# An encoder layer on one core: the pair-wise output projection with squares, root, gate and sums at other steps, and the second FFN product with its left operands in one line and its loads in a set order

## The chip, the cores and the metric

The kernel runs on one core of one Trainium2 chip. A core has five engines that run side by side, each through its own list of instructions in order: TensorE (PE, matmuls; its weight loads are shown apart as PEld), VectorE (DVE), ScalarE (ACT), GpSimd (POOL) and SyncE (SP), which in this kernel issues nearly all transfers between the chip's memory and the on-chip memory. They wait for one another through semaphores. The metric is the device time of one execution in microseconds (us). Before the change it is 2302.77 us, the median of three runs (2301.56 to 2306.2).

## The reference

One layer of a bidirectional encoder over 2048 rows of 1024 numbers, in float32. Cut to the two parts that matter here:

```python
    mix = jnp.concatenate([att, h_m], axis=-1) @ w_out          # output projection
    x = x + gate1 * mix

    hff = rms_norm(x, g_norm2) * (1.0 + scale2) + shift2
    gte, up = jnp.split(hff @ w_ffn_in, 2, axis=-1)             # first FFN product
    ff = (jax.nn.silu(gte) * up) @ w_ffn_out                    # second FFN product
    x = x + gate2 * ff
    return rms_norm(x, g_final)
```

`att` is the attention's output, divided by its root mean square (row by row) ahead of the product; `h_m` is the mLSTM's output times a gate. The inner width of the FFN is 2816.

## The kernel before

Every float32 product is made of three passes of the array: each operand is split into a high part (ACT copies it, rounded) and a low part (DVE subtracts the high part from the original), and `mm3` (lines 55 to 58) issues high x high, high x low and low x high. On top of it the three large products use the Strassen-Winograd scheme: the two operands are cut into 2 x 2 blocks, and seven products of sums of blocks replace eight. The sums are named A11, A12, S1 to S4, A22 on one side and B11, B21, B22, T1 to T4 on the other. Nearly all engine work below is the making of such sums and of their high and low parts, just ahead of the matmuls that use them.

**The order of the work** is written out by hand for the output projection and the first FFN product: inside `manual_schedule` the instructions of an engine stand in the order in which the Python code issues them. The context `rest` holds DVE, ACT, POOL and SP that way; it is closed in the second FFN product, behind the loop of its first product A11. From there on a planner orders these four engines: it may pull an instruction forward when its inputs are ready by its own reckoning. PE keeps its written order to the end (context `hand`).

**The output projection** (loop from line 1439) goes through the 16 row tiles of 128 rows in 8 pairs, p = 0 to 7. For a pair the seven products of 12 matmuls each make 84 matmuls, given out in 28 steps `i` of three (`pull(1)`); product u covers steps 4u to 4u + 3, and when its last matmul is issued DVE adds the result to the residual rows `xr` (line 1178). A bank of products u = 0, 2, 4 and 6 is the same one, likewise that of 3 and 5, so such an addition must be done before the product after the next one may start. Beside the matmuls of a pair (`cur`) the loop does, at set steps: for the following pair (`nxt`) the scaling of the attention rows (`scale`, i = 1), the gate (`gate`, DVE), the sums (`sums`, `s1`, `s4`, POOL), the high parts (`hi`, ACT, at the steps in `HI`) and the low parts (`lo`, DVE, at the steps in `LO`); for the pair after that (`nx2`) the squares of the attention rows (`square`: ACT, then POOL folds them into `msq`), their column sums on PE (`columns`, bank `aps`), the reciprocal root (`rsqrt`, twelve small DVE instructions) and the diagonal matrix from it; and for the finished pair before (`prev`, only for p = 1 to 4) the scaling of its rows with the same root (`prev.scale`, ACT), their transposes on PE (`trn`) at steps 16 to 23 and, for pairs 2 and 3, the sums of the first FFN product's right side (DVE and POOL at steps 20 and 25). `dl` is 1 in pairs 4 and 5, where two instructions of the pair before were put off into this one, and 0 in the others. Behind an `x1` row, `hop_d` and the attention buffer `ma` stand transfers by SP.

**The first FFN product** (`pair`, units n = 0 to 43, two halves of the rows of 22 units each) makes, per unit, seven products of 12 matmuls. Beside product u the generator `weights` makes the next unit's seven weight sums in seven parts; `STEPS[u]` says how many parts are made behind product u. ACT's queue holds, in order, the splits of these parts, the copies of the unit's own banks (`s`, `u`, `c`) and the tanh. Units 0 and 22 start a half; there the right side's last operands are also split beside the products (`finish_op`).

**The second FFN product** (from line 1645) has seven products u in the order A11, S2, S3, A22, S1, S4, A12, each with 11 steps k over the inner width. A step takes one left operand (128 x 1024, loaded from `a_d` by `raw_a`, split by `split_a`, lines 1671 and 1672) and one right operand (`op_w`, POOL sums and a split, lines 1680 and 1681), and has 8 x 3 matmuls into eight banks. The last two steps of a product (seven for A12) are done bank by bank (`tail`), so that DVE can empty one bank after another (`evac`). The left operands live in a ring of four pairs of tiles, so a load waits for the matmuls of the operand four before it. In A11 the loads are written out three ahead (`raw_`), from A11's step 1 on, behind `stores()`, which issues the last five stores to `a_d`; in the other products the code loads an operand where it uses it (`load_a`) and the planner pulls it forward. The weights' blocks come in as W11, W12, W22 and later W21 (`load_w2`, `load_w21`).

In product S1 the residual rows `x1` of one half of the row tiles are loaded (`x1_row`, two tiles) and added (`row0`, line 1811), in S4 those of the other half (`row1`, line 1797), whose rows are then finished: squares, root, two scalings (line 1803) and the store to the output (line 1804). A12's tail finishes the first half's rows (lines 1815 to 1839).

Of the kernel before, what the change touches and what calls it, by code (L numbers as in the profile page):

```python
# [21 lines left out]
P = 128  # L22
T = 2048
D = 1024
# [12 lines left out]
def hybrid_layer_kernel(  # L37
# [1398 lines left out]
    HI, LO = (5, 12, 17, 19, 21, 23, 25), (5, 13, 18, 20, 22, 24, 26)  # L1436
    FIRST = (1, 2, 5, 8, 16, 20, 24)
    rows = None
    for p in range(NPR):
# [15 lines left out]
        for i in range(28):  # L1455
# [27 lines left out]
            if nx2:  # L1483
                if i == 2:
                    sq = [(xd.tile([P, 512], F32, tag="n2", name="msq", bufs=9) if p else
                           w1.tile([P, 512], F32, tag="sq", name="msq")).rearrange("p (k t) -> p k t", k=4) for _ in range(2)]
                    for j in range(2):
                        nx2.square(j, sq[j])
                if i == 8 + dl:
                    ps = bank("a", "aps")  # L1490
                    for j in range(2):
                        columns(ps, j, sq[j])
# [10 lines left out]
            if nx2 and i == 9 + dl:  # L1503
                parts = [(ps[:, :2], 2, 512)] + ([(prev.ssq, 2, D)] if prev else [])
                r = rsqrt(mx, parts, 2 * len(parts), None, f"ar{len(parts)}")
                nx2.diagonal(r, diag())
            if nxt:
                if i == 11:
                    nxt.gate()
                if i == 12:  # L1510
                    nxt.sums(ms2())
                if i == 15:
                    nxt.s1()
                if i == 16:
                    nxt.s4()
            if prev:
                if i == 11:
                    prev.scale(r[:, 2:4])
                prev.step(i)
# [12 lines left out]
    with tc.tile_pool(name="ff", bufs=1, side="right", reuse_waits="tile") as ff:  # L1532
# [91 lines left out]
        for n, (hh, j) in enumerate(units[:-1]):  # L1624
            ws_, turn = nxt_w, n == NJ - 1
            start = lambda u: None
            if turn:
                hop1, finish_op, start = refill_ops(1)
                assert not norms
            STEPS = (0, 0, 0, 2, 2, 1, 2) if n in (0, NJ) else (0, 0, 1, 1, 2, 2, 1)  # L1630

            def beside(u):

                nonlocal nxt_w, raw, more_w
                if n == 0 and u < 3:
                    finish_op(u + 4)
                if n == NJ and u < 2:
                    finish_op(u + 5)
                if turn:
                    if u > 1:  # L1640
                        finish_op(u - 2)
                    return
                if u == 1:
                    more_w = weights(raw)
                for _ in range(STEPS[u]):
                    nxt_w = next(more_w)
                if wseq and (u == 6 and n != NJ - 2 or u == 0 and n == NJ):
                    raw = load_raw(wseq.popleft())
                if n > 1 and u in (1, 3, 5) and norms and next(norms[0], None) is None:
                    norms.popleft()  # L1650

            pair(hh, j, ws_, hop, start, beside)
            if turn:
                hop = hop1
# [29 lines left out]
        W2 = [{}, {}, {}]  # L1684
# [24 lines left out]
        def op_w(u, k):  # L1709
# [8 lines left out]
            if u == "S3":  # L1718
                r = split_w(x1_)
                load_w21(k)  # L1720
                return r
# [9 lines left out]

        def operands(u, k):
            return load_a(u, k), op_w(u, k)

        g2h = wp.tile([P, D], F32, tag="wraw", name="g2h", bufs=1)
        early, raw_, todo_ = [], [], iter(range(KH))

        def split_early():
            k = next(todo_)
            early.append((split_a(*raw_[k]), op_w("A11", k)))  # L1740

        def first_operands(u):

            if u in (1, 3, 5):
                raw_.append(raw_a("A11", len(raw_)))
# [9 lines left out]
        raw_.append(raw_a("A11", 0))  # L1755
# [3 lines left out]
        stores()  # L1759
# [9 lines left out]

        def x1_row(tt, slot):  # L1770
            t = big(slot, "x1r", (P, D), F32)
            sp.dma_start(t, x1_d[tt * P:(tt + 1) * P, :])
            return t
# [18 lines left out]
        def row1(i):  # L1792

            tt = TO[8 * (i // 4) + 4 + i % 4]
            xr = x1_row(tt, i % 2)
            z = rb[i]
            dve.tensor_tensor(z, z, xr, ADD)
# [6 lines left out]
            sp.dma_start(out[tt * P:(tt + 1) * P, :], z)  # L1804
# [3 lines left out]
        def row0(i):  # L1808

            xr = x1_row(TO[8 * (i // 4) + i % 4], i % 2)  # L1810
            dve.tensor_tensor(ra[i], ra[i], xr, ADD)  # L1811
# [32 lines left out]
        for u in ("A11", "S2", "S3", "A22", "S1", "S4", "A12"):  # L1844
# [11 lines left out]
            for k in range(KH - KL):  # L1856
                a, w = early.pop(0) if early else operands(u, k)
                if u == "A11":
                    if k and k + 3 < KH:
                        raw_.append(raw_a("A11", k + 3))  # L1860
                    if k + 2 < KH:
                        load_w2(W12, k + 2)
                    for k_ in (k,) if k < 8 else range(8, KH):
                        load_w2(W22, k_)
# [8 lines left out]
            if u == "A12":  # L1873
                aring.extendleft([("ff", "xt")] * 2 + [("big", f"big{i}") for i in (1, 0, 27, 26, 25, 24)])
            if u == "A11":
                rest.close()
            tail = [early.pop(0) if early else operands(u, k) for k in range(KH - KL, KH)]
            for i in range(8):
                for k, (a, w) in enumerate(tail):
                    mms(i, KH - KL + k, a, w)  # L1880
                evac(u, i, ps[i])
        hand.close()
# [29 lines left out]
```

## Time and profile before

| | |
|---|---|
| median of three runs | 2302.77 us |
| the profiled execution | 2303.92 us |
| its span, first to last instruction | 2302.1 us |
| PE busy | 2230.1 us, 97% of the span, 10822 matmuls |
| DVE busy | 1635.1 us, 71% |
| ACT busy | 1061.6 us, 46% |
| POOL busy | 1057.7 us, 46% |
| output projection, first to last matmul | about 843.7 to 1018.7 us |
| first FFN product | 1018.7 to 1871 us |
| second FFN product | 1871 to 2294 us |

The products of the second FFN product begin at about 1871 (A11), 1931 (S2), 1991 (S3), 2053 (A22), 2113 (S1), 2175 (S4) and 2235 us (A12).

How to read the lines: a row of the order of time has the start, the length, the engine, the line of the kernel, the operation, the tiles as output<-inputs, their shapes and, in brackets, how long the engine had been idle and what ended it. SPq is SP issuing a transfer: the row's length is the issuing, not the transfer. A row of waits has the waiting instruction, what it waited for, and the sum, the number and the longest of these waits. Matmuls overlap in the array: each one lasts about 0.39 us, and they start 0.227 us apart where nothing is missing, so a wait shows as a larger distance between two starts.

### The profile page before, as it was taken

To read this page: it belongs to the slowest core of one execution; us is meant where nothing else is said; L and a number is where in the kernel's file an instruction comes from. 1 tells how busy PE (TensorE), PEld (TensorE's weight loads), DVE (VectorE), ACT (ScalarE), POOL (GpSimd) and SP (SyncE) were. 2 spreads that over 40 slices of the span, in tenths; PEclk is the share of its full clock that TensorE was granted. 3 is DMA by queue.
4 is the path that set the end of the run, shared out by engine and by line. 5 is a ranking of instruction groups with operands and counts; after the bars stand their busy time and mean duration, and the time that the engine had idled before them with its cause. 6 is when DMAs were issued, how large, how long until landed. Compare 5 with 4: busy or idle time off the path is not lost.

```text
span 2302.1 us, 32525 instructions
## 1 busy us (share of the span) xinstructions
PE 2230.1 (97%) x10822; PEld 1859.8 (81%) x10822; DVE 1635.1 (71%) x2995; ACT 1061.6 (46%) x2206; POOL 1057.7 (46%) x876
## 2 busy tenths in 40 slices
PE   6999999999999999999999999999999999999998
PEld 4997778788788878788888888788888878888887
DVE  6787577667687887886667786766666656685694
ACT  5433555545487855444444443533333333233452
POOL 1006534334234343626656666466665654592020
PEclk9999999999999999999999999999999999999999
DMA  8476745577665666863343443533333374443462
GB/s 327 160 246 211 251 149 172 163 220 206 186 186 176 196 213 209 275 247 133 110 148 128 145 160 126 181 118 98 110 105 108 99 266 140 159 155 101 139 218 91
DMA packets 355499, 393.38 MB, mean 171 GB/s; under 512 B 21388, under 2 KB 253180, under 8 KB 355332
## 3 DMA queue, kind: packets, MB, share of 16 engines
q1 hardware_dynamic: 355108, 391.28, 52.3%
q8 instruction: 85, 1.39, 0.2%
q14 instruction: 82, 0.67, 0.1%
q10 hardware_dynamic: 224, 0.04, 0.0%
HBM read 272.05 MB, written 119.19 MB: 170 GB/s over the span
## 4 chain that ended last, share of the span: by engine, by line
PE 51%; DVE 3%; DMA 2%; issue 1%; ACT 1%; POOL 0%; SPq 0%; ACTq 0%; POOLq 0%; DVEq 0%
PE fp L56 12%; PE fp L57 12%; PE fp L58 11%; PE fo L58 5%; PE fo L57 5%; PE fo L56 5%; DMA al<-a_d 1%; PE ops L56 1%; PE ops L57 1%; PE ops L58 1%; DVE al L1672 1%; DVE ra L1811 0%; DVE w L1681 0%; PE trn L166 0%; DMA T<-hop_d 0%
## 5 line engine op out<-in xcount | busy, mean ns | idle before, releaser
L466 PE MATMUL gps<-hT,whi 128*128 128x512 f32 x1088 | 397.5, 419 | 0.3 <-DVE cacc L500 0.3
L57 PE MATMUL fo<-w,ah 128*128 128x512 f32 x616 | 239.9, 389 | 1.9 <-DVE w L1681 1.9
L58 PE MATMUL fo<-w,al 128*128 128x512 f32 x616 | 240.0, 390 | 0.8 <-DVE al L1672 0.8
L56 PE MATMUL fo<-w,ah 128*128 128x512 f32 x616 | 239.8, 389 | 0.0
L466 PE MATMUL gps<-hT,wlo 128*128 128x512 f32 x544 | 228.6, 420 | 0.0
L466 PEld LDWEIGHTS gps<-hT,whi 128*128 128x128 f32 x1088 | 202.0, 191 | 24.5 <-DVE cacc L500 0.7
L56 PE MATMUL fp<-T,S 128*128 128x512 f32 x528 | 206.9, 392 | 2.9 <-ACT s L1568 2.9
L57 PE MATMUL fp<-T,S 128*128 128x512 f32 x528 | 205.7, 390 | 0.0
L58 PE MATMUL fp<-T,S 128*128 128x512 f32 x528 | 205.4, 389 | 0.0
L1672 DVE TENSOR_TENSOR al<-al,ah 128x1024 fp32r<-128x1024 f32 x77 | 120.4, 1568 | 111.0 <-ACT ah L1671 110.9
L1671 ACT ACTIVATE ah<-al 128x1024 fp32r<-128x1024 f32 x77 | 81.7, 1062 | 189.7 <-DMA al<-a_d 185.1
L1411 DVE TENSOR_TENSOR S<-sf,S 128x512 fp32r<-128x512 f32 x86 | 129.4, 1542 | 36.8 <-ACT S L1410 36.6
L1411 DVE TENSOR_TENSOR A<-graw,A 128x512 fp32r<-128x512 f32 x86 | 130.2, 1536 | 16.1 <-ACT A L1410 16.0
L1576 DVE SCALAR_TENSOR_TENSOR g<-t,g 128x512 f32<-128x512 f32 x44 | 44.0, 1000 | 131.0 <-ACT t L1575 131.0
L58 PE MATMUL fp<-B,A 128*128 128x512 f32 x352 | 136.9, 389 | 0.0
L56 PE MATMUL fp<-B,A 128*128 128x512 f32 x352 | 136.9, 389 | 0.0
L57 PE MATMUL fp<-B,A 128*128 128x512 f32 x352 | 136.9, 389 | 0.0
L57 PEld LDWEIGHTS fo<-w,ah 128*128 128x128 f32 x616 | 115.6, 188 | 26.3 <-DVE w L1681 2.2
L58 PEld LDWEIGHTS fo<-w,al 128*128 128x128 f32 x616 | 115.6, 188 | 25.8 <-DVE al L1672 1.7
L56 PEld LDWEIGHTS fo<-w,ah 128*128 128x128 f32 x616 | 115.6, 188 | 24.2 <-ACT w L1680 0.3
L758 POOL TENSOR_SCALAR ap<-ap,adn 128x384 f32<-128x384 f32 (+1 forms) x128 | 73.4, 593 | 125.9 <-DVE adn L756 53.1
L1415 POOL TENSOR_TENSOR sf<-A,A22r 128x512 f32<-128x512 f32 x43 | 59.1, 1374 | 156.1 <-DMA A22r<-in_w_ffn_in_dram 145.7
(419 smaller groups left out, 6201.3 us busy)
## 6 DMA issues: line engine op xcount, KB each, us to landing
al<-a_d SPq DMA_DIRECT2D x77, 512.0 KB, 3.7
wmod<-in_w_mod_dram SPq DMA_DIRECT2D x48, 512.0 KB, 6.8
graw<-in_w_ffn_in_dram SPq DMA_DIRECT2D x43, 512.0 KB, 3.9
a_d<-ka SPq DMA_DIRECT2D x66, 256.0 KB, 4.7
bc<-bc_d SPq DMA_DIRECT2D x64, 256.0 KB, 4.0
hop_d<-n SPq DMA_DIRECT2D x56, 256.0 KB, 4.4
a_d<-u SPq DMA_DIRECT2D x55, 256.0 KB, 4.7
mqk<-qk_d SPq DMA_DIRECT2D x48, 256.0 KB, 4.3
```

The source lines that it names most:

```text
L56: pe.matmul(o, lh, rh, start=first, stop=False, skip_group_check=skip)
L57: pe.matmul(o, lh, rl, start=False, stop=False, skip_group_check=skip)
L58: pe.matmul(o, ll, rh, start=False, stop=last, skip_group_check=skip)
L466: pe.matmul(ps, w[i == 2][:, k, :], hT[n](i == 1, k), start=(k == 0 and i == 0), stop=(k == KT - 1 and i == 2))
L758: pool.tensor_scalar(self.p[g][:, :self.NK], self.p[g][:, :self.NK], dn[:, g:g + 1], 0.0, MUL, ADD)
L1411: dve.tensor_tensor(t[:, 1, :], f, t[:, 0, :].bitcast(F32), SUB)
L1415: pool.tensor_tensor(f1, a21, a22, ADD)
L1576: dve.scalar_tensor_tensor(g0, t0, 1.0, g0, ADD, MUL)
L1671: act.activation(ah, al.bitcast(F32), AF.Copy)
L1672: dve.tensor_tensor(al, al.bitcast(F32), ah.bitcast(F32), SUB)
```

## The change

In the output projection the steps of several helpers are moved; in the first FFN product `STEPS` of units 0 and 22; in the second FFN product the left operands come from one iterator over all products (`line`), fetched by `fetch` at written places, three steps ahead; the W22 loads and the stores of the last unit are moved within A11; SP gets a written order to the end of the kernel (`manual_schedule` on SP behind A11's loop); and for this the loads of W21, the stores of finished rows and the loads of the residual rows, which the code issued from inside their users, are collected and issued by `rows_of` ahead of a step. The number of instructions and of transfers stays as it is.

```diff
-    HI, LO = (5, 12, 17, 19, 21, 23, 25), (5, 13, 18, 20, 22, 24, 26)
+    HI, LO = (5, 14, 18, 20, 22, 24, 26), (5, 14, 19, 21, 23, 25, 27)
...
-                if i == 2:
+                if i == 2 + 4 * dl:
...
                     for j in range(2):
                         nx2.square(j, sq[j])
-                if i == 8 + dl:
+                if i == 8 + 2 * dl:
                     ps = bank("a", "aps")
-                    for j in range(2):
-                        columns(ps, j, sq[j])
+                if i in (8 + 2 * dl, 9 + 2 * dl):
+                    columns(ps, i - 8 - 2 * dl, sq[i - 8 - 2 * dl])
...
-            if nx2 and i == 9 + dl:
+            if nx2 and i == 10 + 2 * dl:
...
-                if i == 11:
+                if i == 12:
                     nxt.gate()
-                if i == 12:
+                if i == 13:
                     nxt.sums(ms2())
-                if i == 15:
+                if i == 16:
                     nxt.s1()
-                if i == 16:
+                if i == 17:
                     nxt.s4()
             if prev:
-                if i == 11:
+                if i == 12:
                     prev.scale(r[:, 2:4])
...
-            STEPS = (0, 0, 0, 2, 2, 1, 2) if n in (0, NJ) else (0, 0, 1, 1, 2, 2, 1)
+            STEPS = (0, 0, 0, 1, 1, 2, 3) if n in (0, NJ) else (0, 0, 1, 1, 2, 2, 1)
...
             if u == "S3":
-                r = split_w(x1_)
-                load_w21(k)
-                return r
+                put_back.append(k)
+                return split_w(x1_)
...
+        US = ("A11", "S2", "S3", "A22", "S1", "S4", "A12")
+        line, raw_ = iter([(u, k) for u in US for k in range(KH)]), deque()
+
+        def fetch(n=1):
+
+            for u, k in islice(line, n):
+                if (u, k) == ("A12", 4):
+                    aring.extendleft([("ff", "xt")] * 2 + [("big", f"big{i}") for i in (1, 0, 27, 26, 25, 24)])
+                raw_.append(raw_a(u, k))
+
         def operands(u, k):
-            return load_a(u, k), op_w(u, k)
+            return split_a(*raw_.popleft()), op_w(u, k)
...
         pair(1, JO[0], nxt_w, hop, then=first_operands)
-        stores()
...
+        def rows_of(u, k):
+
+            while put_back:
+                load_w21(put_back.pop(0))
+            while outs:
+                sp.dma_start(*outs.pop(0))
+            if u in ("S1", "S4"):
+                for i in (0, 1) if k == 0 else (k,) if 1 < k < 8 else ():
+                    x1_row(TO[8 * (i // 4) + 4 * (u == "S4") + i % 4], i % 2)
...
-            sp.dma_start(out[tt * P:(tt + 1) * P, :], z)
+            outs.append((out[tt * P:(tt + 1) * P, :], z))
...
             for k in range(KH - KL):
+                if u != "A11" or k:
+                    fetch(2 if u == "A12" else 1)
+                rows_of(u, k)
                 a, w = early.pop(0) if early else operands(u, k)
                 if u == "A11":
-                    if k and k + 3 < KH:
-                        raw_.append(raw_a("A11", k + 3))
                     if k + 2 < KH:
                         load_w2(W12, k + 2)
-                    for k_ in (k,) if k < 8 else range(8, KH):
+                    if k == 2:
+                        stores()
+                    for k_ in ((), (), (), (0, 1), (2, 3), (4,), (5, 6), (7, 8), (9, 10))[k]:
                         load_w2(W22, k_)
...
             if u == "A11":
                 rest.close()
+                hand.enter_context(tc.manual_schedule(engines={mybir.EngineType.SP}))
+            if u != "A12":
+                fetch()
+            rows_of(u, KH)
             tail = [early.pop(0) if early else operands(u, k) for k in range(KH - KL, KH)]
             for i in range(8):
                 for k, (a, w) in enumerate(tail):
                     mms(i, KH - KL + k, a, w)
                 evac(u, i, ps[i])
+            if u != "A12":
+                fetch()
```

## The prediction made before the run

> **What bounds the kernel now.** I read the page first (TensorE, PE, is busy 97% of the span and the chain that ended last runs through PE for most of its length), then the busy times of chosen stretches, then PE's waits from the output projection on, and last the order of time around each wait. The stretches below are the output projection; the start of the first FFN product; its turn to the second half; product S3 of the second FFN product; its product S4. Columns: stretch, length, then busy time of PE, PE's weight loads, DVE, ACT, POOL.
>
> ```profile
> 843.70:1018.70 175.00, 169.49 (x788) 137.95 (x789) 138.61 (x255) 85.42 (x140) 77.47 (x64) 1.00 0.70 235
> 1018.70:1048.00 29.30, 27.82 (x121) 22.37 (x120) 26.87 (x25) 13.63 (x21) 11.77 (x7) 1.00 0.44 150
> 1447.70:1479.00 31.30, 27.76 (x120) 21.98 (x119) 25.90 (x26) 15.79 (x23) 16.91 (x10) 1.00 0.49 168
> 1991.00:2053.00 62.00, 61.18 (x268) 49.91 (x268) 53.30 (x35) 17.53 (x22) 56.40 (x32) 1.00 0.55 188
> 2173.00:2235.00 62.00, 62.00 (x275) 51.36 (x274) 60.01 (x138) 36.68 (x60) 7.65 (x6) 1.00 0.69 239
> ```
>
> PE is idle 5.5, 1.5, 3.5 and 0.8 us in the first four, and never in S4, where 62.00 us for 275 matmuls give 0.23 us from start to start: that is the pace to beat. All that an edit here can take away are PE's waits after 843.7 us (last column but two: total, times, longest):
>
> ```profile
> PE fp L56 <- ACT s L1568: 2.9, 3, 1.2
> PE aps L1081 <- POOL msq L1033: 2.5, 3, 0.9
> PE fp L56 <- ACT c L1579: 2.1, 2, 1.3
> PE fo L57 <- DVE w L1681: 1.9, 1, 1.9
> PE ops L56 <- DVE xr L1178: 1.8, 3, 0.9
> PE ops L56 <- ACT mA L1070: 1.2, 2, 1.0
> PE fo L58 <- DVE al L1672: 0.8, 2, 0.5
> ```
>
> They sum to 13.2 us of 2302.1. So the change is worth a few us either way; what a measurement can tell from no change is about 0.2%, 4.6 us.
>
> **Second FFN product, first left operands.** The wait of 1.9 us stands here, in product A11 at step 4 (a step is 24 matmuls, 24 x 0.227 = 5.44 us):
>
> ```profile
> 1879.29 1.62 POOL L1613 TENSOR_TENSOR ka<-ka,g 128x512 f32<-128x512 f32 x1
> ...
> 1880.94 0.32 SPq L1545 DMA_DIRECT2D a_d<-ka  x1
> ...
> 1883.27 0.38 SPq L1667 DMA_DIRECT2D al<-a_d  x1
> ...
> 1891.19 1.06 ACT L1671 ACTIVATE ah<-al 128x1024 fp32r<-128x1024 f32 x1 [15.19 <-DMA al<-a_d]
> ...
> 1892.82 0.49 PE L56 MATMUL fo<-w,ah 128*128 128x512 f32 x1
> 1895.24 0.50 PE L57 MATMUL fo<-w,ah 128*128 128x512 f32 x1 [1.92 <-DVE w L1681]
> ```
>
> SP sat in the stores of the last unit until POOL had finished them (1880.9), so the load of step 4's operand went out at 1883.27, landed at 1891.2 (7.9 us) and the split came late: 1895.24 - 1892.82 - 0.23 = 2.2 us lost. The change puts this load ahead of the stores (they move to step 2) and of the W22 loads (the first two go at step 3). Its tile is free when PE ends step 0, at 1892.8 - 3 x 5.44 = 1876.5. The usual time to landing is in this row of the DMA issues (size, median us):
>
> ```profile
> al<-a_d SPq DMA_DIRECT2D x77, 512.0 KB, 3.7
> ```
>
> With 3.7 to 7.9 us the operand is there at 1880 to 1884.5, and with 1.1 us of ACT and at most 4 us of DVE split by 1889.5: **-2.2 us**, from 0 (if DVE, in order, stands behind something else) to -2.2. The W22 loads start some 5 us later than now; they feed the POOL sums of S2, a whole product away. The stores, now behind operand 5 in SP's queue, are read back only at steps 9 and 10; nothing waits.
>
> **The same, later products.** SP gets a set order to the end. Today the planner pulls the residual adds that belong to S1 into S2 and S3, as these rows in order of time show:
>
> ```profile
> 2000.27 2.32 DVE L1811 TENSOR_TENSOR ra<-ra,x1r 128x1024 f32<-128x1024 f32 x1
> 2002.51 2.32 DVE L1672 TENSOR_TENSOR al<-al,ah 128x1024 fp32r<-128x1024 f32 x1
> ```
>
> The add stands ahead of the split that PE waits for (the 0.8 us of the last row of waits). With the x1 loads issued in S1 the adds cannot run in S3: **-0.8 us**. A rule of the Trainium skill bears on this (SBUF — State Buffer, "Who interferes with whom"): a VectorE instruction with two SBUF inputs contends with a GpSimd one that reads SBUF. The 2.32 us here, with POOL busy 56.40 of 62 us, agree; by it the adds get cheaper still in a product without POOL work, which changes nothing in the sum, since DVE does not bind there.
>
> **S4 and the single queue.** This is what the set order can cost. In S4, SP's list per step is now: left operand three ahead, store of row i-2, x1 load of row i. The store waits for the whole row (add, square, root, two scalings), and everything behind it waits too. The rows of today, first the add and the store with first and last start, then the x1 loads' time to landing:
>
> ```profile
> L1797 DVE TENSOR_TENSOR rb<-rb,x1r x8: 1216/1219/1224, 2166.1 to 2202.0; 128x1024 f32<-128x1024 f32 x8
> L1804 SPq DMA_DIRECT2D out_dram<-rb x8: 337/338/338, 2179.2 to 2216.8; - x8
> DMA to landing us min/median/max: 3.8/5.6/8.0
> ```
>
> From add to store it is 13.1 us for the first row and 14.8 for the last, on a DVE that is 97% busy (60.01 of 62.00). Undisturbed it is far less; a half row in the last product's tail:
>
> ```profile
> 2284.62 0.69 DVE L1815 TENSOR_TENSOR ra<-ra,fo 128x512 f32<-128x512 f32 x1 [0.64 <-PE fo L58]
> ...
> 2288.01 0.75 DVE L1838 SCALAR_TENSOR_TENSOR ra<-ra,fry,gfb 128x512 f32<-128x512 f32 x1
> ```
>
> 4.1 us; a whole row has 0.5 more add, some 0.4 more square and a second scaling of 0.75: about 5.8, an estimate from these rows. Call the time from landing to store c. From S4's start the x1 loads of rows 0 and 1 go at 1 us; row 2's load goes behind row 0's store, row 4's behind row 2's, row 6's behind row 4's: at 1 + 3 x 5.6 + 3c = 17.8 + 3c. Behind it stands the last left operand, needed at 9 x 5.44 + 0.7 = 49.7 and landing plus split is 3.7 + 1.1 + 1.2 = 6.0: so it is late once c exceeds **8.6 us**, by 3 us for each us more. c lies between 5.8 and 14.8. I take 9.1, a little under the middle, since part of today's load on DVE are splits for the last product, whose loads now come later: **+1.5 us**, ends 0 and +18.
>
> **The steps of the weights.** In the first unit of each half the splits of the next weights move later (0,0,0,2,2,1,2 to 0,0,0,1,1,2,3), so that DVE's add and ACT's tanh of the unit come ahead of two of them. Two of the three waits of 2.9 us end on the copy s of the following unit, which stands in ACT's queue behind those splits:
>
> ```profile
> 1472.47 1.75 POOL L1422 TENSOR_TENSOR graw<-graw,sf 128x512 f32<-128x512 f32 x1
> ...
> 1475.86 0.58 ACT L1568 ACTIVATE s<-fp 128x512 f32<-128x512 f32 x1
> 1476.49 0.50 PE L56 MATMUL fp<-T,S 128*128 128x512 f32 x1 [1.09 <-ACT s L1568]
> ```
>
> At 1476 POOL ends the last sum at 1474.2; two splits that need it or come behind it, of some 0.5 us each, and then s follow in either order, so s could start at 1475.3 instead of 1475.9 at best. Of the 1.1 us I take 0.3, since a sum of the unit now goes ahead of two of these on POOL. In the first half, where POOL is ahead, I take the whole wait, 2.9 - 1.1 - 1.2 = 0.6 (the third is the turn itself, untouched, and so are the 2.1 us at c): **-0.9 us**, from +0.5 (g of the next unit later) to -1.7.
>
> **Output projection.** A step here is three matmuls, 0.68 us. The column sums are split over two steps, the root comes one step later (two in pairs 4 and 5, where the squares also move four steps), gate, sums, scale one step, and the low halves now stand behind the residual adds on DVE. Rows of pair 4, second column sum, scaling of the rows, their transposes:
>
> ```profile
> 942.07 0.27 PE L1081 MATMUL aps<-ones_r,msq 128*128 128x1 f32 x1 [0.83 <-POOL msq L1033]
> ...
> 945.29 2.19 ACT L1252 ACTIVATE xr<-xr,ar2y 128x1024 f32<-128x1024 f32 x2 [5.24 <-DVE ar2y L106]
> 947.28 0.80 PE L1269 MATMUL trn<-ident,xr 128*128 128x128 f32 x4
> ```
>
> From the column to the scaled rows it is 947.5 - 942.1 = 5.4 us, and the transposes stay at step 16. In pair 4 the second column now stands behind step 11: five steps, 3.4 us, are left, so PE waits 5.4 - 3.4 = 2.0 us there; today it arrives at 947.28, some 0.2 us early: +1.8. In pairs 1 to 3 seven steps, 4.8 us, are left: 0 to 0.6 each, taken as +0.2 in all. In pair 5 the gate comes out about 1 us later against the residual add that PE waits for: +0.8. The waits for msq (2.5) are in pairs 1, 4 and 5: in 4 and 5 the squares go up to four steps later and the columns only one and two, so they keep most of theirs; -1.0, ends 0 and -2.5. The residual adds ahead of the low halves: of the 1.8 + 1.2 us I take -0.7, because the load of a later pair's ma is released by such a low half, and pair 1's columns then wait for it. Sum **+1.1 us**, ends -5.5 (every projection wait gone) and +3.5.
>
> **Sum:** -2.2 - 0.8 + 1.5 - 0.9 + 1.1 = -1.3 us. On the profiled execution's 2303.92 us (span 2302.1, the rest before and after it) that is 2302.6; it lay 1.15 us above the median 2302.77, so of the median **2301.4 us**. Likeliest case alone: 2297.5 to 2306. Chance 0.40.
>
> **Rivals.** (1) **SP's queue in S4 decides.** From c of about 10.5 us the loss there is 5.7 us or more: at 11, 7.2 us instead of 1.5, so 2307.1; at 14.8, 18.6, so 2318.5. For it: the add-to-store times of today; against: the splits of the last product leave DVE. Chance 0.27. In a sentence apart: the Trainium skill (TensorE: Matmul & The Clock Gate, "What's actually happening") has PE fall to half its clock after an idle window of 3.4 us, which would add an estimated 1.7 us to such a stall; no wait here after 843.7 us is that long, and the clock column reads 1.00. (2) **All waits go.** The projection loses its 5.5 us, S4 none: -3.0 - 0.9 - 5.5 = -9.4, so 2293.4; with half of the projection's, 2296. Against it the 5.4 us from column to rows in pair 4. Chance 0.23. (3) **The loads gain nothing**: operand 4 lands in time, but DVE's order lets another split be late, and S3 stays: -0.9 + 1.1 + 1.5 = +1.7, 2304.5; for it, DVE works in order and is busy 53.30 of 62 us in S3. Chance 0.10.
>
> **Numbers.** Faster by over 0.2%: 0.23 of (2) and 0.04 of the likeliest, 0.27. Slower: 0.27 of (1), 0.04 of (3), 0.03 of the likeliest, 0.34. Within: 0.39. The range, 2295.5 to 2311.5, leaves out the ends of (1) and (2).
>
> **What would show it.** Right: no wait of PE at A11's step 4, the operand's load issued near 1876.5; no row add between S2 and S3; a wait of about 2 us at pair 4's first transposes; PE waiting briefly, or not, at S4's tail with the last al load behind a store. Wrong: a wait of over 6 us there (rival 1), no wait at all in the projection (rival 2), or a new wait in S2, A22 or A12, where I see none.

## The result, and the profile after

The changed kernel takes **2313.4 us** in the median of four runs (2313.04 to 2314.46), the kernel before 2302.28 us beside it: a ratio of 1.0046, interval 1.0028 to 1.0063. It is slower by 0.46%; the forecast was 2301.4 us and its range ended at 2311.5. The profiled execution took 2313.04 us (span 2311.3), 9.1 us more than that of before.

To see where, I cut both traces at the first matmul of each stretch. The windows of the changed kernel: projection, then A11, S3, S4 and A12 of the second FFN product (columns as in the prediction; the last three are the granted clock, the DMA share and GB/s).

```profile
845.17:1021.25 176.08, 169.94 (x788) 137.50 (x789) 136.62 (x255) 85.58 (x140) 73.59 (x64) 1.00 0.70 233
1873.01:1932.85 59.84, 59.84 (x266) 49.55 (x264) 39.58 (x32) 17.94 (x23) 46.99 (x27) 1.00 0.65 218
1992.69:2052.53 59.84, 59.84 (x266) 49.55 (x264) 37.01 (x30) 18.61 (x23) 49.27 (x30) 1.00 0.41 137
2172.21:2234.83 62.62, 60.41 (x266) 49.40 (x264) 53.31 (x122) 30.16 (x49) 4.18 (x4) 1.00 0.62 218
2234.83:2303.14 68.31, 63.62 (x265) 51.05 (x263) 46.56 (x108) 25.17 (x43) 7.48 (x5) 0.95 0.32 124
```

And A12 of the kernel before:

```profile
2233.94:2293.99 60.05, 60.05 (x265) 49.35 (x263) 33.50 (x90) 18.78 (x34) 5.33 (x4) 1.00 0.27 97
```

| stretch, us | before | after | difference | forecast |
|---|---|---|---|---|
| ahead of the projection (code unchanged) | 843.7 | 845.2 | +1.5 | 0 |
| output projection | 175.0 | 176.1 | +1.1 | +1.1 |
| first FFN product | 852.4 | 851.8 | -0.6 | -0.9 |
| A11 to S1 | 303.0 | 299.2 | -3.8 | -3.0 |
| S4 | 59.84 | 62.62 | +2.8 | +1.5 |
| A12 | 60.05 | 68.31 | **+8.3** | 0 |

A product that never waits lasts 59.84 us (A12, with the end of its last matmul, 60.05). A11 and S3 reach that now. Most of the loss is in A12, where I saw none. PE's waits from 843.7 us on (total, times, longest) name what it waits for:

```profile
PE fo L56 <- DVE ra L1833: 4.5, 2, 2.4
PE ops L56 <- DVE xr L1178: 4.2, 4, 1.5
...
PE fo L56 <- ACT ah L1671: 1.6, 1, 1.6
PE trn L1269 <- ACT xr L1252: 1.2, 2, 0.7
PE aps L1081 <- POOL msq L1033: 0.8, 2, 0.5
...
PE fo L58 <- DVE al L1672: 0.7, 1, 0.7
```

The two largest `fo` waits end on L1833, the add by which DVE empties one of S4's eight PSUM banks for A12: A12 cannot start in a bank that is still full.

**Where S4 waits: SP's queue.** SP's rows near S4's end, with the store of a row, and the x1 load and the left operand that stand behind it:

```profile
2214.90 0.34 SPq L1790 DMA_DIRECT2D out_dram<-rb  x1
2215.33 0.38 SPq L1783 DMA_DIRECT2D x1r<-x_d  x1
2215.81 0.73 SPq L1667 DMA_DIRECT2D al<-a_d  x1
...
2243.18 0.34 SPq L1790 DMA_DIRECT2D out_dram<-rb  x1
2243.61 4.16 SPq L1667 DMA_DIRECT2D al<-a_d  x7
```

The load at 2215.81 is S4's last operand, 43.6 us into S4 (by the prediction's chain of stores with c = 8.6 it would be 17.8 + 3 x 8.6 = 43.6). It landed 5.5 us later, at 2221.3. On ACT a row's square, which began at 2221.41, stands ahead of its split, and PE waits for both halves of the split:

```profile
2221.41 1.06 ACT L1819 ACTIVATE junk<-rb 128x1024 bf16<-128x1024 f32 x1 [4.86 <-DVE rb L1816]
...
2222.47 1.04 ACT L1671 ACTIVATE ah<-al 128x1024 fp32r<-128x1024 f32 x1
```

```profile
2223.56 0.50 PE L56 MATMUL fo<-w,ah 128*128 128x512 f32 x1 [1.55 <-ACT ah L1671]
2224.95 0.50 PE L58 MATMUL fo<-w,al 128*128 128x512 f32 x1 [0.66 <-DVE al L1672]
2241.88 0.50 PE L56 MATMUL fo<-w,ah 128*128 128x512 f32 x1 [2.38 <-DVE ra L1833]
2245.01 0.79 PE L56 MATMUL fo<-w,ah 128*128 128x512 f32 x1 [2.17 <-DVE ra L1833]
```

**Where A12 waits: DVE.** Row 7's add comes at 2226.5, where the last one came at 2202.0 before. Its root, scalings and the operand splits therefore stand in DVE's list among the adds that empty the banks:

```profile
2226.54 1.23 DVE L1816 TENSOR_TENSOR rb<-rb,x1r 128x1024 f32<-128x1024 f32 x1 [1.31 <-DMA x1r<-x_d]
...
2233.21 2.32 DVE L1672 TENSOR_TENSOR al<-al,ah 128x1024 fp32r<-128x1024 f32 x1
...
2238.28 1.81 DVE L1681 TENSOR_TENSOR w<-w2n,w 128x512 fp32r<-128x512 f32 x1
2240.02 1.21 DVE L1805 SCALAR_TENSOR_TENSOR fry<-fra,fry 128x1 f32<-128x1 f32 x1
2241.15 0.67 DVE L1833 TENSOR_TENSOR ra<-ra,fo 128x512 f32<-128x512 f32 x1
```

The add that PE waits for until 2241.88 begins at 2241.15, behind a step of the root on one column that takes 1.21 us. POOL multiplies beside it:

```profile
2239.81 1.40 POOL L1850 TENSOR_TENSOR ra<-ra,gfb 128x512 f32<-128x512 f32 x1 [0.27 <-ACT junk L1810]
```

From the start of its add to its store a row takes 8 us or so, and the last one twice that (us from S4's start):

```
row       0     1     2     3     4     5     6     7
add      6.6   8.4  20.2  25.6  34.1  39.9  47.9  54.3
store   14.6  17.1  28.9  33.5  42.7  47.3  57.6  71.0
taken    8.0   8.7   8.7   7.9   8.6   7.4   9.7  16.7
```

After the two waits PE's matmuls take twice as long; the windows around them, clock in the last column but two:

```profile
2240.00:2245.00 5.00, 0.96 (x3) 0.48 (x3) 5.00 (x9) 1.50 (x4) 2.77 (x2) 0.89 0.22 83
2245.00:2250.00 5.00, 4.99 (x12) 3.92 (x13) 4.12 (x6) 2.41 (x4) 1.38 (x1) 0.50 0.94 348
```

So of A12's 8.3 us, 68.31 - 63.62 = 4.7 are waits, and 63.62 - 60.05 = 3.6 are slower matmuls.

### The profile page after: what moved, and what is told of

The parts are those of the page before. It is cut to its first block, busy times and chain, and to the rows that moved or that the text cites. A ratio compares the mean times of both kernels' runs of the same rounds, so it can differ in the third digit from the quotient of the medians.

```text
span 2311.3 us, 32505 instructions
## 1 busy us (share of the span) xinstructions
PE 2233.1 (97%) x10822; PEld 1860.8 (81%) x10822; DVE 1625.3 (70%) x2995; ACT 1060.8 (46%) x2206; POOL 1046.2 (45%) x876
## 4 chain that ended last, share of the span: by engine, by line
PE 75%; DVE 10%; DMA 7%; issue 3%; ACT 3%; POOL 2%; SPq 1%; ACTq 0%; POOLq 0%; DVEq 0%
PE fp L56 12%; PE fp L57 12%; PE fp L58 12%; PE gps L466 8%; PE fo L56 5%; PE fo L57 5%; PE fo L58 5%; PE ops L56 2%; PE atp L765 2%; PE ops L58 2%; PE ops L57 2%; DMA x1r<-x_d 1%; PE ao L778 1%; PE as L742 1%; PE as L743 1%
## 5 line engine op out<-in xcount | busy, mean ns | idle before, releaser
L1672 DVE TENSOR_TENSOR al<-al,ah 128x1024 fp32r<-128x1024 f32 x77 | 108.6, 1416 | 111.2 <-ACT ah L1671 111.0
```

Source lines behind the costliest of these rows:

```text
L1672: dve.tensor_tensor(al, al.bitcast(F32), ah.bitcast(F32), SUB)
```

## The experiments

A kernel's time varies over some 9 us from run to run (the kernel before: 2299.4 to 2309.2 beside the first four), mostly ahead of the change: the projection starts between 840.1 and 848.2 us in the traces. The lengths of the products are far steadier, so they decide, and the times confirm. Three theories on S4 and A12: **T**, the store of row i-2 holds SP's loads up; **V**, the rows come too late and crowd DVE where the banks are emptied; **P**, POOL beside them makes DVE's steps long.

**e1: the set order of SP taken away.**

```diff
             if u == "A11":
                 rest.close()
-                hand.enter_context(tc.manual_schedule(engines={mybir.EngineType.SP}))
```

> SP's set order from S2 on is taken away, all else stays: the planner orders SP again. Theory (T, the store of row i-2 stands at the head of SP's queue and holds the loads behind it): S4 and A12 lose their 2.8 and 8.3 us, both within 0.5 us of 59.8, and the wait of S3 comes back (+0.8 to +1.5); time 2302.5 to 2305. Rival (U, the loads in one line three ahead cause the loss, with or without a set order): A12 stays above 64 us; time 2309 or more.

2301.76 us, ratio 0.9993 (0.9982 to 1.0005). S3 and A12:

```profile
1997.25:2058.63 61.38, 60.48 (x266) 49.34 (x264) 51.60 (x34) 17.46 (x23) 56.03 (x31) 1.00 0.54 184
...
2238.15:2298.20 60.05, 60.05 (x265) 49.35 (x263) 34.26 (x92) 19.34 (x36) 7.17 (x5) 1.00 0.26 97
```

S4 is 59.84 again, S3's wait is back with 1.5 us, A11 stays at 59.84. The loss belongs to the set order, not to loads in one line (U falls); what the set order gains by itself is S3's wait alone.

**e2: x1 loads ahead of the stores, each store a step later.**

```diff
-            while outs:
-                sp.dma_start(*outs.pop(0))
             if u in ("S1", "S4"):
...
+            while len(outs) > (u == "S4"):
+                sp.dma_start(*outs.pop(0))
```

> SP's order stays set; in S4 the x1 load of a step goes ahead of the stores, and each store one step (5.4 us) later, row 7's after two of A12's loads. T: no load waits for a row any more, S4 and A12 both 59.8 to 60.3; time 2302 to 2303.5. Rival (V, the x1 loads come in S4 only, so that the adds, roots and scalings of the rows crowd DVE at its tail, whatever the stores do): PE still waits over 3 us in S4's tail and A12; time 2306 to 2311.

2303.95 us, ratio 1.0005 (0.9994 to 1.0015). S4 and A12:

```profile
2171.59:2231.43 59.84, 59.84 (x265) 49.55 (x264) 53.23 (x126) 29.28 (x45) 1.37 (x1) 1.00 0.69 229
2231.43:2294.81 63.38, 61.17 (x265) 49.04 (x263) 43.63 (x104) 25.91 (x48) 11.58 (x7) 1.00 0.36 133
```

T is right for S4, which loses nothing now. A12 still loses 3.3 us, again to L1833: V is right for a part.

**e3: row 7's store alone behind A12's loads.**

```diff
-            while outs:
+            while outs and (u, k) not in (("S4", KH), ("A12", 0)):
```

> Only row 7's store is moved, from ahead of A12's third to eighth left operand to behind its seventh; the stores of rows 0 to 6 stay where they are. T: A12 falls from 68.1 to about 60 us, S4 keeps its 62.6; time 2305 (2304 to 2306.5). V: the chain of row 7 still stands on DVE among the adds that empty S4's banks, so the waits of 2.5 and 2.3 us and the half clock behind them stay; A12 66 us or more, time 2311 to 2313.5.

2309.9 us, ratio 1.0034 (1.0022 to 1.0046).

```profile
2230.76:2297.67 66.91, 63.32 (x265) 51.12 (x263) 45.01 (x107) 24.84 (x43) 6.09 (x5) 0.95 0.34 126
```

T falls for A12: its third operand goes 61 us after S4's start here instead of 71, and yet 6.9 of the 8.3 us stay, the half clock too.

**e4: the projection's edits and the weights' steps alone**, on the kernel before (the diff of the change down to `STEPS`).

> The kernel before with the edits of the output projection and the weights' steps alone; the second FFN product is that of before. By the two traces: projection +1.1 us, first product -0.6 us, second product 303.0 + 59.8 + 59.8 as before; time 2302.3 + 0.5 = 2302.8. Rival (these edits take something in the second product too): its length differs from before by over 1.5 us.

2302.43 us, ratio 0.9998 (0.9987 to 1.0008). S4 and A12 are 59.84 and 60.06 as before, so the loss of the second product is its own. A11 lasts 61.32 and S3 60.31 us, 0.9 and 1.0 less than in the one trace of before, with the same code there. Together that is over the 1.5 us that the rival named, but as a gain. I take it that these two waits vary by about 1 us from run to run; one trace of each kernel does not show it. S3's wait in e1, which has these edits too, is as long as before.

**e5: e2, and the rows of S4 a step earlier.**

```diff
-            if u in ("S1", "S4"):
-                for i in (0, 1) if k == 0 else (k,) if 1 < k < 8 else ():
-                    x1_row(TO[8 * (i // 4) + 4 * (u == "S4") + i % 4], i % 2)
+            if u == "S1" and k < 8:
+                for i in (0, 1) if k == 0 else (k,) if 1 < k < 8 else ():
+                    x1_row(TO[8 * (i // 4) + i % 4], i % 2)
+            if (u, k) == ("S1", KH) or u == "S4" and 0 < k < 7:
+                for i in (0, 1) if u == "S1" else (k + 1,):
+                    x1_row(TO[8 * (i // 4) + 4 + i % 4], i % 2)
...
-                if u == "S4" and 0 < k <= 8:
-                    row1(k - 1)
+                if u == "S4" and k < 8:
+                    row1(k)
```

> The order of e2 (x1 loads ahead of the stores, each store a step later), and rows 0 and 1 of S4 are loaded at S1's end, every other row one step (5.4 us) earlier, and so its add, root and scalings. Theory V (what is left in e2, 3.3 us in A12, is the chain of the last rows on DVE among the adds that empty S4's banks): A12 at 60.1, S4 at 59.8; time 3 us under e2, near 2300.5. Rival P (POOL's multiplications beside those adds hold DVE up, wherever the rows stand): A12 62 us or more.

2300.26 us, ratio 0.9982 (0.9973 to 0.9991). A12 waits for nothing:

```profile
2231.05:2291.10 60.05, 60.05 (x265) 49.35 (x263) 39.22 (x96) 23.64 (x40) 7.68 (x5) 1.00 0.37 141
```

V is right, and P alone is not enough: POOL makes the same multiplications here.

**e6: the changed kernel with only the rows a step earlier** (the diff of e5 without that of e2).

> The changed kernel with the rows a step earlier as in e5, and the stores where the change has them, ahead of the loads. If the store ahead of the loads and the row's lateness act together (T and V): the last store goes near 2236 instead of 2243, S4 at 59.8 to 60.4, A12 at 60 to 62.5. If the store's place alone decides (T): A12 64 us or more.

2303.27 us, ratio 1.000 (0.999 to 1.001).

```profile
2172.05:2233.07 61.02, 60.42 (x266) 49.39 (x264) 54.60 (x129) 29.64 (x48) 3.66 (x3) 1.00 0.64 215
2233.07:2295.10 62.03, 60.38 (x265) 49.23 (x263) 40.81 (x99) 23.78 (x42) 8.17 (x6) 1.00 0.34 128
```

One step of 5.4 us takes most of A12's loss away with the stores where the change has them. The last row's store goes 53.8 us after S4's start, at 2225.9, not near 2236; the sizes of S4 and A12 are about those that T and V together expect (S4 0.6 over).

**e7: the changed kernel without POOL's multiplication beside the emptying.**

```diff
-                pool.tensor_tensor(a[:, M[1]], a[:, M[1]], gfb[1], MUL)
```

> The changed kernel without the multiplication by gfb of one half of each row that POOL makes beside the adds that empty S4's banks (this part of the computation is left out). P: without it DVE's small steps there, 1.2 us each beside POOL, take 0.15 to 0.7 us, and A12 falls from 68.3 to 62 or less with all stores and rows as they are. T and V: A12 keeps 65 us or more, S4 its 62.6.

2304.3 us, ratio 1.0003 (0.9993 to 1.0013), with that part of the work left out.

```profile
2169.36:2234.28 64.92, 61.99 (x265) 50.52 (x264) 55.06 (x133) 32.35 (x55) 0.00 (x0) 0.97 0.62 211
2234.28:2294.34 60.06, 60.06 (x265) 49.35 (x263) 37.38 (x97) 23.22 (x39) 0.00 (x0) 1.00 0.37 141
```

P's forecast for A12 holds fully: 60.06 us, although the rows are as late as in the changed kernel (row 7's store goes 66.3 us after S4's start instead of 71.0). S4 keeps SP's loss and more (5.1 us: 2.3 us of waiting for the last operand, then its low half, and a lower clock behind), so S4 and A12 together are 6.0 us shorter than in the changed kernel, not 8.3. The longer S4 gave DVE 2.3 us more, but the last bank's add ends 67.0 us after S4's start, and with the changed kernel's S4 it would be needed at about 62.6 + 7 x 0.68 = 67.4 (an estimate from these rows). The wait in S4:

```profile
2221.42 0.50 PE L56 MATMUL fo<-w,ah 128*128 128x512 f32 x1 [2.27 <-ACT ah L1671]
```

DVE's groups from 2215 to 2250 us, first of the changed kernel, then of e7 (busy, mean ns of one):

```profile
L1849 DVE TENSOR_TENSOR fssq<-fssq,deps 128x1 f32<-128x1 f32 x8 | 3.3, 419 | 0.1
L1681 DVE TENSOR_TENSOR w<-w2n,w 128x512 fp32r<-128x512 f32 x2 | 2.5, 1246 | 0.0
```

```profile
L1681 DVE TENSOR_TENSOR w<-w2n,w 128x512 fp32r<-128x512 f32 x2 | 1.4, 684 | 0.0
...
L1849 DVE TENSOR_TENSOR fssq<-fssq,deps 128x1 f32<-128x1 f32 x8 | 1.2, 156 | 0.1
```

These steps, with both inputs in SBUF, are 1.8 and 2.7 times as long on the mean beside POOL. Put together, A12's loss follows the time at which row 7's add starts (us from S4's start; S4's first bank is full some 50 us in, and the chain behind the add is about 8.5 us long):

```
kernel                    row 7's add    A12 over 60.05
before                       27.9            0
e5                           42.3            0
e6                           46.4            2.0
e2                           48.9            3.3
e3                           52.2            6.9
changed                      54.3            8.3
e7 (no POOL beside it)       54.9            0
```

**e8: e5 with the projection of before.**

> e5 with the output projection of before. Projection 1.1 us shorter than in e5 (175.0 to 175.9), first product as changed (851.8), second product 7 x 59.84 + 0.2; against before -2.4 -1.5 -0.5 = -4.4 us: 2298.5, ratio 0.998. Rival (the projection's length is moved by the edits no more than by chance): it lies within 0.5 us of e5's, and the time 2299.5.

**2295.21 us, ratio 0.9969 (0.9957 to 0.9981)**: faster than both kernels. The projection, and A11 to S4 with no wait at all (6 x 59.84 = 359.04):

```profile
841.05:1014.90 173.85, 169.14 (x789) 138.00 (x789) 137.33 (x254) 85.39 (x140) 76.75 (x64) 1.00 0.70 237
...
1864.21:2223.25 359.04, 359.04 (x1586) 297.30 (x1584) 238.65 (x292) 123.88 (x161) 146.19 (x86) 1.00 0.48 159
```

The projection is 2.8 us shorter than e5's 176.65, where 1.1 was expected; the first product, 849.31 us, is shorter than expected too, and the time lies 3.3 us under the expected one. Over all traces it is 176.1 to 177.8 us with the change's edits (eight traces) and 173.9 to 175.0 without (three): they cost about 2.4 us, more than the two first traces showed.

**e9 and e10: one half of the projection's edits each, on e8.** e9 has squares, columns, root and scale of the change, e10 the low halves, gate and sums.

```diff
 e9
-                if i == 2:
+                if i == 2 + 4 * dl:
...
+                if i in (8 + 2 * dl, 9 + 2 * dl):
+                    columns(ps, i - 8 - 2 * dl, sq[i - 8 - 2 * dl])
...
-            if nx2 and i == 9 + dl:
+            if nx2 and i == 10 + 2 * dl:
...
-                if i == 11:
+                if i == 12:
                     prev.scale(r[:, 2:4])
 e10
-    HI, LO = (5, 12, 17, 19, 21, 23, 25), (5, 13, 18, 20, 22, 24, 26)
+    HI, LO = (5, 14, 18, 20, 22, 24, 26), (5, 14, 19, 21, 23, 25, 27)
...
-                if i == 11:
+                if i == 12:
                     nxt.gate()
```

> e8 with one half of the projection's edits back: squares four steps later in pairs 4 and 5, column sums over two steps, root one step later (two in pairs 4 and 5), rows' scale one step later; the low halves, gate and sums as in e8. Theory (the root is late in pair 4): pair 4 lasts 25.5 us as with all edits, against 23.53 in e8; pair 1 22.9 and pair 5 23.1 as in e8; about 2 us over e8's projection. Rival (the low halves, gate and sums behind the residual adds are the cost): pair 4 at 23.5.

> e8 with the other half back: low halves behind the residual adds, gate, sums and the two Strassen sums a step later; squares, columns and root as in e8. Theory: pair 4 stays at 23.5, pair 1 goes up by 0.6 us to 23.5, pair 5 by 0.2. Rival: pair 4 at 25 or more, pair 1 at 22.9.

e9: 2312.46 us, ratio 1.004 (1.0025 to 1.0055); e10: 2302.47 us, 1.0003 (0.9993 to 1.0012). Lengths of the pairs:

```
           pair 0   pair 1   pair 4   pair 5   projection
before      22.68    23.11    23.53    23.09     175.02
changed     21.01    23.55    25.57    23.31     176.08
e5          21.54    23.70    25.47    23.29     176.65
e8          21.83    22.85    23.53    23.06     173.85
e9          22.61    26.86    28.27    22.94     190.00
e10         21.77    24.20    25.27    24.38     178.72
e12         21.10    23.55    26.28    24.01     177.71
```

None of the four expectations holds in full (e10's rival has pair 4 right and pair 1 wrong): the halves are not additive, each alone costs more than both (e10 by only about 1 us, in single traces). In e9 PE's waits for the transposes, `trn`, sum to 11.1 us, where the changed kernel has 1.2. The rows' scale stands behind the high half of step 12 on ACT, which waits for the gate (the row names PE, but the gate's DVE instruction, L1051, ends at 880.32, just ahead of it):

```profile
880.40 0.63 ACT L1070 ACTIVATE mA<-mm 128x512 fp32r<-128x512 f32 x1 [7.57 <-PE ops L58]
880.94 2.17 ACT L1252 ACTIVATE xr<-xr,ar2y 128x1024 f32<-128x1024 f32 x2
```

In the change that half is at step 14, behind the scale; so it seems to be the later high halves that make the later scale bearable. In e10, where the columns are not moved, PE waits for the sums of the squares instead:

```profile
PE aps L1081 <- POOL msq L1033: 4.3, 4, 1.3
```

**e11: the last unit's stores first, the weights' steps of before, on e8.**

```diff
-            STEPS = (0, 0, 0, 1, 1, 2, 3) if n in (0, NJ) else (0, 0, 1, 1, 2, 2, 1)
+            STEPS = (0, 0, 0, 2, 2, 1, 2) if n in (0, NJ) else (0, 0, 1, 1, 2, 2, 1)
...
         pair(1, JO[0], nxt_w, hop, then=first_operands)
+        stores()
...
-                    if k == 2:
-                        stores()
```

> e8 with the last unit's stores back ahead of A11's later left operands (the W22 loads stay where the change has them), and the weights' steps of before. Theory (the operand's load stood behind the stores): A11 61.3 to 62.2 us instead of 59.84, and the first FFN product waits 0.85 us again 25.3 us after its start, which no kernel with the changed steps did. Rival (the W22 loads were what held the operand up): A11 stays at 59.84.

2300.43 us, ratio 0.9992 (0.9981 to 1.0002). The rival is right on A11, which stays at 59.84; the first product waits 0.83 us again 25.4 us after its start. SP and the split of step 4's operand (A11 starts at 1869.54):

```profile
1879.40 0.32 SPq L1545 DMA_DIRECT2D a_d<-ka  x1
...
1881.26 0.38 SPq L1667 DMA_DIRECT2D al<-a_d  x1
```

```profile
1887.89 1.06 ACT L1671 ACTIVATE ah<-al 128x1024 fp32r<-128x1024 f32 x1 [15.24 <-DMA al<-a_d]
...
1890.13 0.68 DVE L1681 TENSOR_TENSOR w<-w2x,w 128x512 fp32r<-128x512 f32 x1
```

The load goes 11.7 us after A11's start, against 12.2 before, behind the same stores. But without the W22 loads around it, it lands in 6.6 us, not 7.9, and the split of the weight takes 0.68 us, not 1.76: ready at 1890.8, needed at 1869.54 + 4 x 5.44 = 1891.3. The longer split stood beside POOL, in the kernel before:

```profile
1892.38 2.25 POOL L1715 TENSOR_TENSOR w2n<-w2y,w2n 128x512 f32<-128x512 f32 x1 [0.91 <-DMA w2y<-in_w_ffn_out_dram]
1893.42 1.76 DVE L1681 TENSOR_TENSOR w<-w2x,w 128x512 fp32r<-128x512 f32 x1
```

This sum of POOL's waits for a W22 load; in e11 the first one begins at 1893.05, after the split. So about 1.1 of the 2.8 us by which the split ends earlier (counted from A11's start) is the same contention as in A12. An `x1` load that the planner had pulled forward to 1888.05 is gone in e11 too, and is not told apart from the W22 loads. The time, 0.9992, is nearer to the kernel before than e8's 0.9969; the projection and the first product are 2.5 us longer here than in e8's trace, about half of that, so a part of e8's gain may be chance.

**e12: e5 without the further delay in pairs 4 and 5.**

```diff
-                if i == 2 + 4 * dl:
+                if i == 2:
...
-                if i in (8 + 2 * dl, 9 + 2 * dl):
-                    columns(ps, i - 8 - 2 * dl, sq[i - 8 - 2 * dl])
+                if i in (8 + dl, 9 + dl):
+                    columns(ps, i - 8 - dl, sq[i - 8 - dl])
...
-            if nx2 and i == 10 + 2 * dl:
+            if nx2 and i == 10 + dl:
```

> e5, in pairs 4 and 5 of the projection without the further delay: squares at step 2 as in the other pairs (not 6), column sums at steps 9 and 10 (not 10 and 11), root at 11 (not 12). Theory (the late squares and root cost pair 4 its 2 us): pair 4 at 23.5 to 24.0 us instead of 25.5, pair 1 unchanged at 23.6. Rival (e9 and e10 show that the order of all the parts together counts, low halves and gate too): pair 4 stays at 25 or more.

2301.33 us, ratio 0.9994 (0.9984 to 1.0004). Pair 4 is 26.28 us, longer, not shorter; the rival holds. The root stands in DVE's order behind a residual add that waits for PE, as it does in the changed kernel (at 944.54, after 1.97 us):

```profile
943.04 0.69 DVE L1178 TENSOR_TENSOR xr<-xr,ops 128x512 f32<-128x512 f32 x1 [1.82 <-PE ops L58]
943.64 0.15 DVE L99 TENSOR_SCALAR ar2v<-aps 128x2 f32<-128x2 f32 x1
```

The theory that the delay as such costs pair 4 its 2 us falls.

## Why the prediction was wrong

**The step that failed** is "S4 and the single queue". It followed one thing through SP's queue, S4's last left operand, and closed with no loss in A12; its list of what would prove it wrong names "a new wait in S2, A22 or A12, where I see none". The same queue also makes the rows late, and I did not carry that on: row 7's chain runs into the emptying of S4's banks, and PE waits in A12 for the adds queued behind it: 8.3 us where I had none. Rows a step earlier take this away, wholly in e5 and down to 2.0 us in e6; e2 and e3, which move stores, leave 3.3 and 6.9. Its sentence that the last product's splits "leave DVE" in S4 was true (DVE is busy 53.31 us there, not 57.85) and of little use, since two of them, 4.1 us beside POOL, stand among the same adds.

**The rule that I put in the wrong place.** The Trainium skill (SBUF — State Buffer, "Who interferes with whom") was weighed for S3 only, and set aside because DVE does not bind there. In S4's tail DVE does bind: in e7, without POOL beside them, the same late rows cost A12 nothing. It also bore on A11's wait, where POOL's sum stood beside the split (e11).

**What S4 itself showed** was the queue forecast, with the terms mis-sized: +2.8 us for +1.5. The queue's order was right, with the last operand issued 43.6 us in. But c was 7.9 to 8.7 us for the rows ahead of it, less than the 9.1 I took and about the limit of 8.6 or under it: by my sum S4 would have lost next to nothing. The loss came from the term behind c. The operand landed in 5.5 us, beside the x1 load just ahead of it, and a row's square held its split on ACT for another 1.2, so the split starts 2222.47 - 2215.81 = 6.7 us after the issue, where I had 3.7. That +1.5 came near +2.8 is luck.

**Rival 1** had the place in code and the sign, and its times (2307 to 2318.5) hold the result; but it too put the loss on S4's last operand, which made 2.8 of 11.0 us. It was nearer for a reason it does not give. Its sentence on the half clock assumed one long wait; the clock fell after two shorter ones, and cost 3.6 us, not 1.7.

**A11**, -2.2: measured -2.4, but the cause given, SP sitting in the stores, is not needed: e11 keeps the stores first and loses nothing. What made the operand late enough were the loads beside it and POOL's sum beside the split; that moving the W22 loads suffices I did not see, and no run moves the stores alone. **S3**, -0.8: measured -1.5; e1 brings it back with the planner's order, so the cause is right and the size lies within this wait's variation (0.5 us in e4). **The steps of the weights**, -0.9: measured -0.6; e11 brings back the wait of 0.8 us in the first half. The second half's wait is 0.98 us after 1.09 in the first two traces, but 0 to 1.0 over the twelve traces with the changed steps, so its part is not settled; the whole product varies from 849.3 to 852.2 us over those twelve, and lasts 851.2 (e11) and 852.4 us with the steps of before.

**Output projection**, +1.1: measured +1.1 in the two traces, but its terms were not. Waits for the columns -1.7 (I had -1.0), transposes of pair 4 +1.2 (+1.8). The residual adds took +2.4: 0.9 in pair 5, where I had +0.8, and a new wait of 1.5 in pair 4, which I did not see; the -0.7 that I took off these adds and the high halves together had the wrong sign. The sum agreed by luck, because pair 0, which varies from 21.0 to 22.7 us over the traces, was 1.7 us shorter in this one. Which of its edits costs pair 4 most is left open: e9, e10 and e12 only show that their effects do not add.

## What to carry to other kernels

In a queue with a set order, follow everything that stands behind a waiting instruction to its last user: here the operand that I followed lost 2.8 us, and the row loads beside it lost 8.3 in the next product. Work that fills gaps on an engine should be finished before that engine has to empty the accumulators: with POOL at work beside it, a last row add 42 us into the product was free, at 46 us it cost 2.0 and at 54 us 8.3 (without POOL, 55 us was free). Put loads for later steps ahead of a store that waits for a computation, and let the store go a step late (e2, e5).

## What the runs showed of the hardware

**DVE beside POOL.** A DVE step on one column with both inputs in SBUF (L1805 above) took 1.21 us beside POOL's multiplication, and L1849 took 0.156 us on the mean in e7, without it; an add with one input in PSUM (L1833) stayed at 0.67. So a tiny step can cost as much as a large one (an add of 128x1024, L1816, took 1.23 without POOL). This agrees with the Trainium skill (SBUF — State Buffer, "Who interferes with whom"); these numbers are what it means for a chain of small steps.

**The clock halves without a long wait.** PE's longest wait here was 2.38 us, yet after two of them within 6 us the clock went to 0.50, and stayed there across the window from 2245 to 2250. In 2240 to 2245 PE was busy for 0.96 of 5 us. In e7 waits of 2.27 and 0.66 us were followed by a mean clock of 0.80 from 2225 to 2230. The single wait of 1.92 us in the kernel before (A11, step 4) left it at 1.00:

```profile
1893.00:1898.00 5.00, 3.08 (x13) 2.27 (x14) 5.00 (x4) 2.16 (x3) 4.92 (x3) 1.00 1.03 408
```

The Trainium skill (TensorE: Matmul & The Clock Gate, "What's actually happening") puts the fall after an idle window of about 3.4 us; by these rows a window with a few matmuls in it is enough.
